# A residual block with attention and RWKV-7 time mixing: the recurrent part's two-operand multiplies move from GpSimd to VectorE, small copies to ScalarE, and the scheduler counts both

## The chip, the core and the metric

The kernel runs on one core of a Trainium2 chip. A core has five engines with queues of their own: TensorE (PE in the profile; PEld is its weight load), VectorE (DVE), ScalarE (ACT), GpSimd (POOL) and SyncE (SP), which here issues all DMA transfers. The metric is the device time of one execution in microseconds (us); smaller is better.

## The reference

One layer over 1024 tokens of 1024 channels, all in float32. The part that the change touches is the time mixing `rwkv7_time_mix`, 8 heads of 64 channels:

```python
def step(state, inp):                       # one token, one head
    r_t, w_t, k_t, v_t, kk_t, a_t = inp
    sa = einsum('bhvk,bhk->bhv', state, -kk_t)
    state = state * w_t + outer(sa, kk_t * a_t) + outer(v_t, k_t)
    return state, einsum('bhvk,bhk->bhv', state, r_t)

kk = k * k_k;  kk = kk / max(norm(kk), 1e-12)
k  = k * (1 + (a - 1) * k_a)
y  = (normalised scan output) * lnx_w + lnx_b
out = (y + bonus) * g
```

Around it stand a norm and an input projection, stick-breaking attention (8 heads; `q`, `k`, `v` from the same projection), sigmoid gates that merge the two branches, an output projection, and a SwiGLU FFN with 2816 hidden channels, each with a norm.

## The kernel before

Every matrix product is done as three products of float32r parts (high by high, high by low, low by high), so TensorE's work is large: most of it is a 128x128 weight block times 128x512 activations. Several products are done in Strassen's form, which adds sums of blocks on VectorE.

**The recurrence in chunks.** The 1024 tokens are cut into chunks of 64. Heads are handled in four pairs p (a pair fills 128 partitions) and the tokens in two halves hf of 8 chunks; one (p, hf) is called a unit here, and there are eight. For each unit `rw_elementwise` makes, on tiles of 128 partitions by 512 tokens, the running decay products `pp` and their inverses `pinv`, the normalised key `kk`, `ar` (kk and r times the decay) and `bk` (kk times a, and k', over the decay), and then the chunk matrices `nx` by small matmuls (64 rows by 128 columns; PE `e_e<-b_ar,b_bk`). Of each chunk a triangular 64x64 matrix has to be inverted, `rw_inverse`:

1. its 32x32 diagonal blocks go to DRAM (`nd`, 8 DMAs) and come back spread over partitions (`nl`);
2. VectorE inverts them in 16 pairs of a multiply and a reduce, the recursion (`b_tmp<-b_nl,q_q` and `q_q<-b_tmp`);
3. the result `ts` goes to DRAM in four DMAs (`td`) and comes back as `dn` (`q_q<-td`);
4. TensorE makes the off-diagonal block with two small products of 32x32 blocks, `ph` (`y_y<-q_q,b_nx`) and `pt` (`y_y<-q_q,q_q`); between them `ph` is copied from PSUM to `hb` (`COPY q_q<-y_y`).

I call these two the first and the second inverse product. `rw_chain` then carries the state from chunk to chunk: PE `c_c<-b_sv,b_nx`, ACT `b_xv<-c_c`, PE `c_c<-b_xv,b_bkt`, DVE `b_sv<-c_c,pl_pl,sp_sp`, where POOL makes `sp` (`sp_sp<-b_sv,pl_pl`, the decayed state) ahead of it. `rw_post` normalises a unit's output and multiplies it by the gate `g`. In attention, `values` makes differences `dv` of neighbouring values, and GpSimd masks each score block (`TENSOR_SCALAR_AFFINE_SELECT`) before VectorE's scan.

**Who sets the order.** Every operation is first recorded by `Block.record`, so the profile puts nearly all of them on one line, L610. Then `Block.schedule` simulates the five engines with a table of costs (`cost`), of latencies from engine to engine (`LATENCY`, and `MARGIN` for another engine), and of the times that transfers take beyond a fixed one (`LANDS`), and issues each engine's operations in the order that results. The chip keeps each engine's order and waits where the plan was wrong. Priorities are the order of recording with offsets: `CHAIN` for the state chain, `INV` for the inverse; projections of the next pair, attention and gates fill TensorE in between. `WB` and `PREFETCH` say how far ahead of its turn a tile may be granted. A two-input operation of VectorE or GpSimd on SBUF is made to end later when the other engine is in such an operation (`self.turn`); before, only `tensor_tensor` and `scalar_tensor_tensor` count.

Of the kernel before, what the change touches and what calls it, by code (L numbers as in the profile page):

```python
# [9 lines left out]
AF = mybir.ActivationFunctionType  # L10
ALU = mybir.AluOpType
# [4 lines left out]
P = 128  # L16
# [3 lines left out]
H = 512  # L20
# [12 lines left out]
WO_CLS = ("raw", "raw", "whi", "whi", "wlo", "wlo", "b", "b")  # L33
BY_OUT = (6, 5)
FIFTH = 0
INV = -100
AWAKE = (9, 8)
TQ = S // 4
POST = 0
# [2 lines left out]
SUMS_AT, OSPLIT = None, 1  # L42
MPS_A, MPS_S = "dydy", "ecec"
SBW = ("whi", "b", "wlo", "b")
WB, WP, WS, RB = 60, 8, 4, 2
PREFETCH = 14
CH = 64
RMS_EPS = 1e-6
GN_EPS = 64 * 1e-5
# [39 lines left out]
def is_ap(x):  # L89
    return hasattr(x, "tensor") and hasattr(x, "offset") and hasattr(x, "ap")  # L90
# [50 lines left out]
def cost(engine, method, kw, in_psum):  # L141

    out = kw.get("out", kw.get("ap"))
    if out is None:
        return 1283.0
    n = count(out.shape[1:])
    if engine == "tensor":
        if method == "transpose":
            return 2 + max(out.shape[0], n) / 1.2
        m, full = count(kw["lhsT"].shape[1:]), kw["lhsT"].dtype == F32  # L150
        if out.shape[0] <= CH and n <= CH:
            return 59.0 if out.shape[0] == CH else 27.0
        if full and kw["lhsT"].shape[0] == CH:
            return 122.0
        return 2 * (2 + max(m, n) / 1.2) if full else max(m / 2.4, 1.5 + 0.4435 * n)
    psum = any(is_ap(v) and k not in OUTS and in_psum(v) for k, v in kw.items())
    if engine == "vector":
        if method == "tensor_copy" and not psum:
            return 60 + 0.52 * n
        if method == "tensor_reduce":  # L160
            n = count(kw["in_"].shape[1:])
            return 64 + 1.042 * n
        if method == "scalar_tensor_tensor":
            return max(196, 68 + (1.16 if psum else 1.1) * n)
        if method == "tensor_tensor_scan":
            return 60 + 2.083 * n
        if method == "tensor_tensor" and abs(kw["in0"].ap[-1][0]) > 16:
            return 68 + 1.8 * n
        return 68 + 1.042 * n
    if engine == "scalar":  # L170
        extra = "accum_out" in kw or any(is_ap(kw.get(k)) for k in ("scale", "bias"))
        return 55 + 0.833 * n + (0 if psum else 40) + (90 if extra else 0)
    if engine == "gpsimd":
        if method == "memset":
            return 98 + 0.8 * n
        if method == "tensor_copy":
            return 180 + 3.4 * n
        if method == "tensor_scalar":
            return 320 + 2.4 * n
        return 150 + 2.1 * n  # L180
    size = 4 * count(out.shape)
    return max(450.0, size / 360.0)

LANDS = {"nd": -800.0, "nl": 1000.0, "td": -400.0, "tl": 800.0, "xv": 600.0, "spill": 1700.0, "gate": 2200.0, "act": 900.0, "x2": 1900.0, "orw": 1000.0, "w_rw": 1500.0, "w_sb": 1000.0, "w_fu": 1000.0, "w_fg": 500.0}


HELD, HEAD = 115.0, 140.0
POINTERS = ("scale", "bias", "scalar", "scalar1", "scalar2")  # L190
# [72 lines left out]
    "gpsimd": {"tensor": 155, "vector": 100, "scalar": 80, "gpsimd": 105, "sync": 60},  # L263
    "sync": {"tensor": 2030, "vector": 2030, "scalar": 2030, "gpsimd": 2060, "sync": 2030},
}
MARGIN = 80
CHAIN = -1000
SOON = -(10**7)

# [5 lines left out]
class Block:  # L275
# [150 lines left out]
    def schedule(self):  # L426

        import heapq

        for op in self.ops:  # L430
            op.ready = 0.0
            op.need = len(op.preds)
            op.left = op.need + len(op.tiles)
            for q in op.preds:
                q.succs.append(op)
        free = {e: 0.0 for e in ENGINES}
        self.begin, self.turn = {}, {}
        waiting = {e: [] for e in ENGINES}
        able = {e: [] for e in ENGINES}

        def release(op):
            ready = op.ready
            if op.bundle:
                op.bundle.left -= 1
                if op.bundle.left:
                    return
                ready = max(q.ready for q in op.bundle.ops)
                op = op.bundle.ops[0]
            heapq.heappush(waiting[op.engine], (ready, op.prio, op.seq, op))

        def advance(op):
            for q in self.want(op):
                release(q)

        for op in self.ops:
            if not op.left:
                release(op)
        for op in self.ops:
            if not op.need:
                advance(op)  # L460
        done = []
        last = None
        while len(done) < len(self.ops):
            best = None
            for e in ENGINES:
                if able[e]:
                    at = free[e]
                elif waiting[e]:
                    at = max(free[e], waiting[e][0][0])
                else:  # L470
                    continue
                if best is None or at < best[0]:
                    best = (at, e)
            if best is None:

                self.forced = False
                forced = [q for cls in self.places.values() for q in self.grant(cls, True)]
                assert self.forced, "the tiles do not fit"
                for q in forced:
                    release(q)  # L480
                continue
            at, e = best
            while waiting[e] and waiting[e][0][0] <= at:
                _, p, q, op = heapq.heappop(waiting[e])
                heapq.heappush(able[e], (p, q, op))
            op = self.choose(able[e], waiting[e], at, last)
            if op is None:
                free[e] = waiting[e][0][0]
                continue
            for op in op.bundle.ops if op.bundle else (op,):  # L490
                at, last = self.run(op, e, at, last, free, done, release, advance)
        return done
# [13 lines left out]
    def run(self, op, e, at, last, free, done, release, advance):  # L506
# [11 lines left out]
            last = op  # L518
        op.start = at
        op.end = at + op.cost  # L520
        if e in ("vector", "gpsimd") and op.method in ("tensor_tensor", "scalar_tensor_tensor") and not self.in_psum(op.kw["in0"]) and not self.in_psum(op.kw["in1"]):

            other = self.turn.get("gpsimd" if e == "vector" else "vector", 0.0)
            if other > at:
                op.end = max(op.end, other + op.cost - HEAD)
            self.turn[e] = op.end
        free[e] = op.end
        done.append(op)
        for q in op.succs:
            q.ready = max(q.ready, op.end + op.late + wait(e, q.engine))  # L530
# [6 lines left out]
        for tile in op.tiles:  # L537
            tile.left -= 1
            tile.ends[e] = max(tile.ends.get(e, 0.0), op.end)
            if not tile.left:  # L540
# [614 lines left out]
def rw_elementwise(b, u, p, hf, spill):  # L1155
    nc = b.nc
# [6 lines left out]
    def c8(t):  # L1163
        return t.rearrange("p (c t) -> p c t", c=8)
# [30 lines left out]
    ar = T("b", [P, 8, P], F32, "ar")  # L1195
    bk = T("b", [P, 8 * P], F32, "bk").rearrange("p (c a t) -> p c a t", c=8, a=2)
    nc.vector.scalar_tensor_tensor(out=ar[:, :, 0:CH], in0=c8(kk), scalar=-1.0, in1=pp[:, :, 0:CH], op0=ALU.mult, op1=ALU.mult)
    nc.gpsimd.tensor_tensor(out=ar[:, :, CH:P], in0=c8(r), in1=pp[:, :, 1 : CH + 1], op=ALU.mult)
    nc.gpsimd.tensor_tensor(out=kk[:], in0=kk[:], in1=a[:], op=ALU.mult)
    for h, rs in enumerate(halves):  # L1200
        nc.vector.tensor_tensor(out=bk[rs, :, h, :], in0=c8(kk)[rs], in1=c8(pinv)[rs], op=ALU.mult)

    nc.vector.tensor_scalar(out=a[:], in0=a[:], scalar1=pc(PC_KA + p), scalar2=oka[:, p : p + 1], op0=ALU.mult, op1=ALU.add)
    kp = a
    nc.gpsimd.tensor_tensor(out=kp[:], in0=k[:], in1=a[:], op=ALU.mult)
    for h, rs in enumerate(halves):
        nc.vector.tensor_tensor(out=bk[rs, :, 1 - h, :], in0=c8(kp)[rs], in1=c8(pinv)[rs], op=ALU.mult)

# [77 lines left out]
def rw_inverse(b, nd, nx, quads, tinit, p, hf):  # L1286

    nc = b.nc
# [42 lines left out]
        for c, h in ((c, h) for c in range(8) for h in range(2)):  # L1331
            nc.tensor.matmul(ph[bot[h], c, :], lhsT=nx[c // 4][top[h], c % 4, 0, h, 32:CH], rhs=dn[top[h], c, :], start=True, stop=True)
    for h in range(2):
        nc.vector.tensor_copy(hb[bot[h]], ph[bot[h]])
    pt = T("y", [P, 8, 32])
    with b.together():
        for c, h in ((c, h) for c in range(8) for h in range(2)):
# [47 lines left out]
def rw_post(b, y, u, p, hf, spill):  # L1385
    nc = b.nc
    T = b.t
    pc, ones = b.pc, b.ones
    t0 = T("b", [P, H], F32, "ptmp")
    nc.scalar.activation(t0[:], y[:], AF.Square)  # L1390
    pn = T("c", [P, H])
    nc.tensor.matmul(pn[:], lhsT=ones, rhs=t0[:], start=True, stop=True)
    rs = T("b", [P, H], F32, "ptmp")
    nc.scalar.activation(rs[:], pn[:], AF.Ln, scale=1.0 / CH, bias=b.eps[:, 1:2])
    nc.scalar.activation(rs[:], rs[:], AF.Exp, scale=-0.5)
    nc.vector.scalar_tensor_tensor(out=rs[:], in0=y[:], scalar=pc(PC_LW + p), in1=rs[:], op0=ALU.mult, op1=ALU.mult)
    nc.vector.scalar_tensor_tensor(out=rs[:], in0=rs[:], scalar=pc(PC_LB + p), in1=u["bv"][:], op0=ALU.add, op1=ALU.add)
    g = T("b", [P, H], F32, "ptmp")
    nc.sync.dma_start(g[:], spill["g"][:])
    b.ops[-1].late = LANDS["spill"]  # L1400
    nc.gpsimd.tensor_tensor(out=rs[:], in0=rs[:], in1=g[:], op=ALU.mult)
    nc.sync.dma_start(b.orw_d[p][:, hf * H : hf * H + H], rs[:])


# [19 lines left out]
def att_inputs(b, p):  # L1424
# [33 lines left out]
    def values():  # L1458
# [3 lines left out]
        for hf in range(2):  # L1462
# [6 lines left out]
            nc.scalar.copy(vt[:, 1 : H + 1], ps)  # L1469
            nc.gpsimd.tensor_copy(ends[0][:, 4 * hf : 4 * hf + 4], vt[:, P : H + 1 : P])  # L1470
            dv = T("b", [P, H], F32, "dv")
            nc.gpsimd.tensor_tensor(out=dv, in0=vt[:, 0:H], in1=vt[:, 1 : H + 1], op=ALU.subtract)
            pv = T("c", [P, 4, P])
            for i in range(4):
                nc.tensor.transpose(pv[:, i, :], dv[:, i * P : i * P + P], b.ident)
# [693 lines left out]
```

## Time and profile before

| | us |
|---|---|
| median of three runs (1549.14 to 1551.74) | 1549.5 |
| profiled execution, its own time | 1552.13 |
| its span, first to last instruction | 1550.3 |
| PE busy in the span | 1523.1 (98%) |
| DVE busy | 1290.0 (83%) |
| ACT busy | 795.1 (51%) |
| POOL busy | 218.2 (14%) |

The profiled execution lies 2.63 us above the median. A busy PE may still hold short waits between pipelined matmuls, so the rows on waits and the idle time ahead of single instructions say more than the 98%. By time: input norm to about 40 us, projections and the first units to 140, the recurrence with filler to about 440, attention to 640, then merge, output projection and FFN. Times in rows of the timeline are us from the span's start; what stands in brackets is the engine's idle time ahead of the row and what ended it.

### The profile page before, as it was taken

To read this page: it belongs to the slowest core of one execution; us is meant where nothing else is said; L and a number is where in the kernel's file an instruction comes from. 1 tells how busy PE (TensorE), PEld (TensorE's weight loads), DVE (VectorE), ACT (ScalarE), POOL (GpSimd) and SP (SyncE) were. 2 spreads that over 40 slices of the span, in tenths; PEclk is the share of its full clock that TensorE was granted. 3 is DMA by queue.
4 is the path that set the end of the run, shared out by engine and by line. 5 is a ranking of instruction groups with operands and counts; after the bars stand their busy time and mean duration, and the time that the engine had idled before them with its cause. 6 is when DMAs were issued, how large, how long until landed. Compare 5 with 4: busy or idle time off the path is not lost.

```text
span 1550.3 us, 24590 instructions
## 1 busy us (share of the span) xinstructions
PE 1523.1 (98%) x8957; PEld 1253.8 (81%) x8957; DVE 1290.0 (83%) x2218; ACT 795.1 (51%) x1623; POOL 218.2 (14%) x387
## 2 busy tenths in 40 slices
PE   8999999999999999999999999999999999999998
PEld 7877777778887888788888887888888888888886
DVE  7769898888686989985999789889889899976684
ACT  7634554555576677523656686233333334554351
POOL 1032355443523132000100000000000000000000
PEclk9999999999999999999999999999999999999999
DMA  9733332321010024543651532443232333964562
GB/s 363 265 92 83 90 101 75 100 83 49 28 42 27 28 68 144 189 142 125 211 170 58 194 135 71 148 166 119 76 129 83 110 115 118 351 217 130 166 214 109
DMA packets 116969, 200.88 MB, mean 130 GB/s; under 512 B 42992, under 2 KB 48368, under 8 KB 116848
## 3 DMA queue, kind: packets, MB, share of 16 engines
q1 hardware_dynamic: 116848, 199.30, 38.6%
q8 instruction: 71, 1.16, 0.3%
q14 instruction: 50, 0.41, 0.1%
HBM read 145.52 MB, written 51.64 MB: 127 GB/s over the span
## 4 chain that ended last, share of the span: by engine, by line
PE 84%; DVE 8%; DMA 3%; issue 2%; ACT 2%; POOL 1%; SPq 0%; DVEq 0%; POOLq 0%; ACTq 0%
PE d_d L610 27%; PE e_e L610 23%; PE c_c L610 18%; PE y_y L610 16%; DVE b_tmp L610 1%; DVE q_q L610 1%; DMA q_q<-td 1%; POOL sp_sp L610 1%; DVE big_h L610 1%; DVE b_xt L610 1%; DMA q_q<-consts 0%; DVE b_full L610 0%; SPq L610 0%; DMA b_nl<-nd 0%; DMA td<-q_q 0%
## 5 line engine op out<-in xcount | busy, mean ns | idle before, releaser
L610 PE MATMUL d_d<-big_h,whi_whi 128*128 128x512 f32 x832 | 286.1, 412 | 0.0
L610 PEld LDWEIGHTS d_d<-big_h,whi_whi 128*128 128x128 f32 x832 | 151.7, 189 | 30.1 <-issue 3.6
L610 PE MATMUL d_d<-big_h,wlo_wlo 128*128 128x512 f32 x416 | 170.1, 409 | 0.1
L610 DVE TENSOR_TENSOR_SCAN b_nb<-b_nb 128x128 f32<-128x128 f32 (+3 forms) x64 | 87.3, 1380 | 5.7 <-POOL b_nb L610 5.0
L610 PEld LDWEIGHTS d_d<-big_h,wlo_wlo 128*128 128x128 f32 x416 | 78.5, 189 | 16.1 <-issue 1.7
L610 POOL TENSOR_SCALAR sp_sp<-b_sv,pl_pl 64x64 f32<-64x64 f32 x120 | 71.7, 598 | 77.8 <-DVE b_sv L610 71.6
L610 PE MATMUL e_e<-big_h,b_a 128*128 128x512 f32 x264 | 67.6, 395 | 0.1
L610 PE MATMUL e_e<-big_h,whi_a 128*128 128x512 f32 x264 | 66.7, 395 | 0.8 <-ACT b_u L610 0.8
L610 PE MATMUL d_d<-b_wd,big_act 128*128 128x512 f32 x264 | 66.6, 394 | 0.0
L610 PE MATMUL e_e<-b_wd,big_act 128*128 128x512 f32 x264 | 66.3, 394 | 0.0
L610 PE MATMUL e_e<-big_h,wlo_a 128*128 128x512 f32 x264 | 66.1, 393 | 0.0
L610 ACT CAST b_wd<-b_wraw 128x512 fp32r<-128x512 f32 x65 | 38.1, 619 | 44.7 <-DVE b_wraw L610 22.9
L610 DVE TENSOR_TENSOR b_wt<-c_c,b_wt 128x512 fp32r<-128x512 f32 (+2 forms) x96 | 50.1, 546 | 10.5 <-ACT b_wt L610 8.9
L610 PEld LDWEIGHTS e_e<-b_wd,big_act 128*128 128x128 f32 x264 | 49.5, 188 | 11.5
L610 PEld LDWEIGHTS d_d<-b_wd,big_act 128*128 128x128 f32 x264 | 49.4, 188 | 11.5
L610 PEld LDWEIGHTS e_e<-big_h,whi_a 128*128 128x128 f32 x264 | 48.9, 188 | 12.0 <-ACT b_u L610 1.2
L610 PEld LDWEIGHTS e_e<-big_h,b_a 128*128 128x128 f32 x264 | 49.0, 188 | 11.6 <-ACT b_a L610 0.5
L610 PEld LDWEIGHTS e_e<-big_h,wlo_a 128*128 128x128 f32 x264 | 49.0, 188 | 10.5
L610 ACT COPY b_xv<-c_c 64x64 f32<-64x64 f32 x128 | 26.4, 206 | 57.5 <-PE c_c L610 56.2
L610 DVE TENSOR_TENSOR b_wd<-b_wraw,b_wd 128x512 fp32r<-128x512 f32 x65 | 42.3, 684 | 13.8 <-ACT b_wd L610 13.7
L610 PE MATMUL d_d<-big_h,whi_a 128*128 128x512 f32 x204 | 53.4, 398 | 0.0
L610 PE MATMUL d_d<-big_h,b_a 128*128 128x512 f32 x204 | 52.6, 397 | 0.4 <-ACT b_g L610 0.4
(898 smaller groups left out, 3982.4 us busy)
## 6 DMA issues: line engine op xcount, KB each, us to landing
raw_raw<-w_in SPq DMA_DIRECT2D x43, 512.0 KB, 3.8
raw_raw<-w_fg SPq DMA_DIRECT2D x26, 512.0 KB, 3.5
b_wraw<-w_fd SPq DMA_DIRECT2D x22, 512.0 KB, 4.8
act<-b_sa SPq DMA_DIRECT2D x32, 256.0 KB, 2.1
b_b<-w_fu SPq DMA_DIRECT2D x16, 512.0 KB, 4.3
b_x<-x SPq DMA_DIRECT2D x14, 512.0 KB, 6.3
act<-b_u SPq DMA_DIRECT2D x28, 256.0 KB, 2.3
raw_araw<-act SPq DMA_DIRECT2D x14, 512.0 KB, 4.0
```

Of the source, the lines that this page charges most:

```text
L610: getattr(getattr(self.real, op.engine), op.method)(**kw)
```

## The change

It does four things. The elementwise multiplies with two SBUF operands that GpSimd did in a unit (`ar`, `kk*a`, `k*a`), the last multiply of `rw_post` and the difference `dv` are issued on VectorE. A scaling of `a` by two per-partition numbers goes from VectorE to ScalarE, and so do the two `hb` copies of a unit. The planner's rule for GpSimd beside VectorE now also takes VectorE's scans as two-input operations and makes GpSimd's `tensor_scalar`, `tensor_copy` and `affine_select` end later beside one. SyncE's queue is modelled by an issue time (`ISSUE`) apart from the time in which transfers pass one after the other (`self.moved`). Some constants change with it.

```diff
-INV = -100
+INV = -300
-WB, WP, WS, RB = 60, 8, 4, 2
-PREFETCH = 14
+WB, WP, WS, RB = 50, 8, 4, 2
+PREFETCH = 13
...
         if method == "tensor_copy":
-            return 180 + 3.4 * n
+            return 180 + 0.84 * n
+        if method == "affine_select":
+            return 165 + n
...
-LANDS = {"nd": -800.0, "nl": 1000.0, "td": -400.0, "tl": 800.0, "xv": 600.0, ...
+LANDS = {"nd": -800.0, "nl": 1100.0, "td": -500.0, "tl": 800.0, "xv": 1050.0, ...
+ISSUE = {0.0: 500.0, LANDS["nd"]: 420.0, LANDS["td"]: 650.0, LANDS["xv"]: 750.0, LANDS["nl"]: 650.0}
...
-MARGIN = 80
+MARGIN = 100
...
-        if e in ("vector", "gpsimd") and op.method in ("tensor_tensor", "scalar_tensor_tensor") and not self.in_psum(op.kw["in0"]) and not self.in_psum(op.kw["in1"]):
-            other = self.turn.get("gpsimd" if e == "vector" else "vector", 0.0)
-            if other > at:
-                op.end = max(op.end, other + op.cost - HEAD)
-            self.turn[e] = op.end
+        if e in ("vector", "gpsimd"):
+            pair = self.paired(op)
+            if pair or e == "gpsimd" and op.method in ("tensor_scalar", "tensor_copy", "affine_select"):
+                other = self.turn.get("gpsimd" if e == "vector" else "vector", 0.0)
+                if other > at:
+                    op.end = max(op.end, other + op.cost - HEAD)
+                if pair:
+                    self.turn[e] = op.end
         free[e] = op.end
+        if e == "sync":
+            self.moved = max(self.moved, at) + op.cost
+            op.end = self.moved
+            free[e] = at + ISSUE.get(op.late, ISSUE[0.0])
...
+    def paired(self, op):
+        ins = [op.kw.get(k) for k in ("in0", "in1", "data0", "data1")]
+        return sum(is_ap(v) and not self.in_psum(v) for v in ins) == 2
...
-    nc.gpsimd.tensor_tensor(out=ar[:, :, CH:P], in0=c8(r), in1=pp[:, :, 1 : CH + 1], op=ALU.mult)
-    nc.gpsimd.tensor_tensor(out=kk[:], in0=kk[:], in1=a[:], op=ALU.mult)
+    nc.vector.tensor_tensor(out=ar[:, :, CH:P], in0=c8(r), in1=pp[:, :, 1 : CH + 1], op=ALU.mult)
+    nc.vector.tensor_tensor(out=kk[:], in0=kk[:], in1=a[:], op=ALU.mult)
...
-    nc.vector.tensor_scalar(out=a[:], in0=a[:], scalar1=pc(PC_KA + p), scalar2=oka[:, p : p + 1], op0=ALU.mult, op1=ALU.add)
+    nc.scalar.activation(a[:], a[:], AF.Identity, scale=pc(PC_KA + p), bias=oka[:, p : p + 1])
-    nc.gpsimd.tensor_tensor(out=kp[:], in0=k[:], in1=a[:], op=ALU.mult)
+    nc.vector.tensor_tensor(out=kp[:], in0=k[:], in1=a[:], op=ALU.mult)
...
-        nc.vector.tensor_copy(hb[bot[h]], ph[bot[h]])
+        nc.scalar.copy(hb[bot[h]], ph[bot[h]])
...
-    nc.gpsimd.tensor_tensor(out=rs[:], in0=rs[:], in1=g[:], op=ALU.mult)
+    nc.vector.tensor_tensor(out=rs[:], in0=rs[:], in1=g[:], op=ALU.mult)
...
-            nc.gpsimd.tensor_tensor(out=dv, in0=vt[:, 0:H], in1=vt[:, 1 : H + 1], op=ALU.subtract)
+            nc.vector.tensor_tensor(out=dv, in0=vt[:, 0:H], in1=vt[:, 1 : H + 1], op=ALU.subtract)
```

Since the order of every engine comes out of the plan, nearly all rows move. Three places are shown, all around the fifth unit (p = 2, hf = 0), which lies near 290 us in the profile before.

GpSimd there, before: `b_sh` is the tile of `tt`, `b_ptmp_3255` the output of `rw_post`, the other TENSOR_TENSOR rows are `ar`, `kk*a` and `k*a` of the last two units.

```order
L610 TENSOR_TENSOR b_ptmp_3255<-b_ptmp_3255,b_sh_1975 128x512
L610 COPY b_sh_2239<-q_q_3273 32x8x32 x3
L610 COPY pl_pl_3381<-b_pp_3253 128x8
L610 TENSOR_TENSOR b_ar_3444<-b_pp_2418,b_pp_3253 128x8x64
L610 TENSOR_TENSOR b_ar_3454<-b_tmp_1433,b_pp_3281 128x8x64
L610 TENSOR_TENSOR b_tmp_1433<-b_tmp_1433,b_pp_972 128x512
L610 TENSOR_SCALAR sp_sp_3495<-b_sv_2421,pl_pl_2459 64x64 x2
L610 TENSOR_TENSOR b_pp_972<-b_pp_972,b_tmp_3279 128x512
L610 TENSOR_SCALAR sp_sp_3517<-b_sv_2421,pl_pl_2459 64x64 x2
```

GpSimd at the same place, after:

```order
L624 COPY pl_pl_3199<-b_ptmp_976 128x8
L624 COPY carry_carry_3236<-b_ptmp_2312 128x1
L624 COPY b_a_662<-carry_carry_3236 128x1
L624 COPY b_ptmp_2304<-q_q_3266 32x8x32 x4
L624 MEMSET b_sv_3331 64x64 x2
L624 TENSOR_SCALAR sp_sp_3443<-b_sv_2607,pl_pl_2426 64x64 x2
```

The multiplies are gone from between the `sp` of the state chain: GpSimd's program goes from 44 TENSOR_TENSOR to 4.

VectorE there, before: the end of the next unit's recursion (`b_nl`), with the `hb` copies in it.

```order
L610 TENSOR_TENSOR b_tmp_2450<-b_nl_3073,q_q_2454 128x14x28
L610 COPY q_q_3384<-y_y_3311 32x256 x2
L610 TENSOR_REDUCE q_q_2454<-b_tmp_2450 128x7x2
L610 SCALAR_TENSOR_TENSOR b_pp_972<-b_pp_2418,par_par_158,b_pp_3253 128x512
L610 TENSOR_TENSOR b_tmp_2450<-b_nl_3073,q_q_2454 128x16x30
```

VectorE at the end of that recursion, after:

```order
L624 SCALAR_TENSOR_TENSOR b_ar_3245<-b_pp_2338,b_ptmp_976 128x8x64
L624 TENSOR_TENSOR b_sh_3028<-b_nl_3079,q_q_2364 128x14x28
L624 TENSOR_TENSOR b_pp_2338<-b_pp_2338,b_xl_600 128x512
L624 TENSOR_REDUCE q_q_2364<-b_sh_3028 128x7x2
L624 TENSOR_SCALAR b_sh_3028<-e_e_3408 128x512
L624 SCALAR_TENSOR_TENSOR b_sv_2607<-c_c_3420,pl_pl_2426,sp_sp_2863 64x64 x2
L624 TENSOR_TENSOR b_sh_3028<-b_nl_3079,q_q_2364 128x16x30
L624 TENSOR_TENSOR b_xl_600<-b_ptmp_2323,b_xl_600 128x512
```

The copies have left; the multiplies `kk*a` (`b_pp_2338`) and `k*a` (`b_xl_600`) stand between the steps of the recursion.

ScalarE and TensorE at the two inverse products, after; ScalarE first. `b_nx<-b_ar` are copies that may start only when the first inverse product has read `nx`.

```order
L624 COPY b_nx_2817<-b_ar_2441 64x4x64 x2
L624 COPY b_nx_2861<-b_ar_2441 64x4x64
L624 COPY q_q_3339<-y_y_3300 32x256 x2
L624 COPY b_xv_2686<-c_c_3337 64x64 x2
L624 COPY b_nx_2861<-b_ar_2441 64x4x64
```

```order
L624 MATMUL y_y_3300<-q_q_3266,b_nx_2861 32x32 x8
L624 MATMUL e_e_3293<-cst_cst_156,b_sh_2991 128x128
L624 MATMUL d_d_3286<-big_h_239,whi_whi_3178 128x512 x2
L624 MATMUL d_d_3286<-big_h_239,wlo_wlo_3225 128x512
L624 MATMUL c_c_3337<-b_sv_2607,b_nx_2817 128x128
L624 MATMUL d_d_3286<-big_h_239,whi_whi_3178 128x512 x2
L624 MATMUL d_d_3286<-big_h_239,wlo_wlo_3225 128x512
L624 MATMUL d_d_3286<-big_h_239,whi_whi_3178 128x512 x2
L624 MATMUL y_y_3353<-q_q_3339,q_q_3317 32x32 x16
```

The `hb` copies (`q_q_3339`) now stand in ScalarE's queue behind three of the `nx` copies, and eight products 512 wide lie between the two inverse products; before there are 23. Over the eight units these are 117 before and 54 after. Between a unit's last `nx` product and its first inverse product there are 1037 products 512 wide before, over the eight units, and 1021 after.

More of the change, by code (lines that the diff above doesn't have):

```diff
@@ L182, in cost @@
     return max(450.0, size / 360.0)
-LANDS = {"nd": -800.0, "nl": 1000.0, "td": -400.0, "tl": 800.0, "xv": 600.0, "spill": 1700.0, "gate": 2200.0, "act": 900.0, "x2": 1900.0, "orw": 1000.0, "w_rw": 1500.0, "w_sb": 1000.0, "w_fu": 1000.0, "w_fg": 500.0}
+LANDS = {"nd": -800.0, "nl": 1100.0, "td": -500.0, "tl": 800.0, "xv": 1050.0, "spill": 1700.0, "gate": 2200.0, "act": 900.0, "x2": 1900.0, "orw": 1000.0, "w_rw": 1500.0, "w_sb": 1000.0, "w_fu": 1000.0, "w_fg": 500.0}
+ISSUE = {0.0: 500.0, LANDS["nd"]: 420.0, LANDS["td"]: 650.0, LANDS["xv"]: 750.0, LANDS["nl"]: 650.0}
 HELD, HEAD = 115.0, 140.0
@@ L436, in schedule @@
         free = {e: 0.0 for e in ENGINES}
-        self.begin, self.turn = {}, {}
+        self.begin, self.turn, self.moved = {}, {}, 0.0
         waiting = {e: [] for e in ENGINES}
```

## The prediction

> **What bounds the kernel.** I read the page first: engines, then the chain that ended last, then the stretches of time, and there TensorE's waits.
>
> ```profile
> span 1550.3 us, 24590 instructions
> PE 1523.1 (98%) x8957; PEld 1253.8 (81%) x8957; DVE 1290.0 (83%) x2218; ACT 795.1 (51%) x1623; POOL 218.2 (14%) x387
> PE 84%; DVE 8%; DMA 3%; issue 2%; ACT 2%; POOL 1%; SPq 0%; DVEq 0%; POOLq 0%; ACTq 0%
> ```
> Stretch by stretch, the columns are the length and then the busy time of PE, PEld, DVE, ACT and POOL with their instructions, PE's granted clock, the share of the DMA engines and GB/s:
>
> ```profile
> 0.00:40.00 40.00, 34.58 (x236) 30.14 (x237) 31.97 (x65) 28.63 (x50) 7.08 (x20) 0.96 0.94 353
> 140.00:440.00 300.00, 290.15 (x2868) 233.61 (x2867) 250.46 (x532) 161.55 (x415) 140.31 (x251) 1.00 0.27 75
> 440.00:640.00 200.00, 195.58 (x1162) 167.09 (x1161) 174.32 (x230) 139.97 (x303) 45.06 (x67) 0.99 0.19 62
> 640.00:1325.00 685.00, 684.06 (x3252) 566.29 (x3251) 600.78 (x1037) 314.67 (x598) 6.45 (x4) 1.00 0.40 134
> 1325.00:1550.30 225.30, 218.80 (x964) 177.81 (x962) 158.69 (x237) 101.06 (x177) 0.00 (x0) 0.99 0.56 195
> ```
>
> TensorE bounds everything. The change leaves its instructions as they are, so only idle time can be won: 1550.3 - 1523.1 = 27.2 us. Of that 5.4 us lie in the first 40 us and 6.5 us after 1325 (the last results leaving), where the change moves nothing of weight. What is left is 9.9 us in the recurrence, 4.4 us in attention and 1.0 us elsewhere. VectorE is at 250 of 300 us in the recurrence, so it has room; GpSimd, idle by its total, is at 140 of 300 there.
>
> TensorE's waits by what ended them (total us, times, longest) say where the 15 us come from:
>
> ```profile
> PE c_c L610 <- DVE b_sv L610: 3.4, 4, 1.4
> PE y_y L610 <- DMA q_q<-td: 3.4, 3, 1.4
> PE y_y L610 <- DVE b_wt L610: 1.3, 2, 1.1
> PE y_y L610 <- DVE q_q L610: 1.3, 2, 1.1
> PE d_d L610 <- ACT b_g L610: 1.3, 2, 0.8
> PE e_e L610 <- ACT b_u L610: 0.8, 1, 0.8
> PE e_e L610 <- DVE q_q L610: 0.8, 1, 0.8
> PE e_e L610 <- DVE b_tmp L610: 0.7, 1, 0.7
> PE c_c L610 <- POOL b_nb L610: 0.6, 1, 0.6
> PE c_c L610 <- DVE b_nb L610: 0.5, 1, 0.5
> ```
>
> **Why GpSimd's multiplies are behind some of them.** Two places in the timeline, with TensorE's wait at the end of each:
>
> ```profile
> 288.75 1.58 DVE L610 TENSOR_TENSOR b_tmp<-b_nl,q_q 128x264 f32<-128x264 f32 x1
> 288.77 1.26 POOL L610 TENSOR_TENSOR b_ptmp<-b_ptmp,b_sh 128x512 f32<-128x512 f32 x1
> ...
> 295.62 0.86 DVE L610 COPY q_q<-y_y 32x256 f32<-32x256 f32 x2
> ...
> 296.63 0.69 PE L610 MATMUL y_y<-q_q,q_q 32*32 32x32 f32 x32 [1.09 <-DVE q_q L610]
> ```
> ```profile
> 334.22 1.65 DVE L610 TENSOR_TENSOR b_tmp<-b_nl,q_q 128x4 f32<-128x4 f32 x1
> 334.57 1.28 POOL L610 TENSOR_TENSOR b_sh<-b_sh,b_tmp 128x512 f32<-128x512 f32 x1
> ...
> 336.74 0.49 PE L610 MATMUL e_e<-b_ar,b_bk 64*128 64x128 f32 x4 [0.78 <-DVE q_q L610]
> ```
>
> A VectorE multiply of four elements a lane takes 1.65 us because a GpSimd multiply of 1.28 us runs beside it. Both engines lose, and all that stands behind in VectorE's queue is late: the `hb` copies at 295.62, for which TensorE waits 1.09 us. In the timeline I find 19 VectorE instructions longer than their kind beside such a GpSimd TENSOR_TENSOR; over the usual length they lose 14.8 us (the first and the last):
>
> ```profile
> 95.95 1.13 DVE L610 SCALAR_TENSOR_TENSOR b_ar<-b_r,b_sh 128x512 f32<-128x512 f32 x1
> ...
> 562.77 2.13 DVE L610 TENSOR_TENSOR b_a<-raw_raw,b_a 128x512 fp32r<-128x512 f32 x2
> ```
>
> **The change, part by part.** Durations for it, from the groups of instructions:
>
> ```profile
> L610 DVE TENSOR_TENSOR b_nl<-b_nl,b_tmp 128x512 f32<-128x512 f32 x4 | 2.7, 686 | 0.1
> L610 DVE TENSOR_SCALAR b_tmp<-b_tmp,par_par,small_small 128x512 f32<-128x512 f32 x2 | 1.1, 546 | 0.1
> L610 DVE COPY q_q<-y_y 32x256 f32<-32x256 f32 x16 | 6.8, 424 | 0.4
> ```
> ```profile
> L610 ACT COPY b_nx<-b_ar 64x256 f32<-64x256 f32 x32 | 12.9, 403 | 12.9 <-PE y_y L610 12.4
> L610 ACT COPY b_sh<-y_y 32x256 f32<-32x256 f32 x6 | 2.2, 364 | 2.4 <-PE y_y L610 2.3
> L610 ACT ACTIVATE b_sh<-c_c,small_small 128x512 f32<-128x512 f32 x2 | 1.4, 676 | 0.3 <-PE c_c L610 0.3
> ```
> ```profile
> L610 POOL TENSOR_SCALAR sp_sp<-b_sv,pl_pl 64x64 f32<-64x64 f32 x120 | 71.7, 598 | 77.8 <-DVE b_sv L610 71.6
> ```
>
> *VectorE's load.* It gains 40 operations (8 units with 3 multiplies, 8 last multiplies, 8 `dv`) of 0.686 us, 27.4 us. It loses 8 scalings of 0.546 (4.4 us) and the 16 `hb` copies (6.8 us). That is +16.2 us, against 14.8 us of stretching that ends: about even, +1.4 us. If a strided multiply ran like the stretched 1.13 us above, the 40 would cost 45 us; the unstretched 0.69 is nearer, as nothing on GpSimd with two operands is left beside it.
>
> *ScalarE's load.* 8 scalings at 0.676 (the nearest row with two pointer operands; it reads PSUM, and the 0.62 to 0.75 of its neighbours are the ends) and 16 copies at 0.364: 11.2 us, in a stage where ScalarE is busy 162 of 300 us.
>
> *Waits that go.* Those that I can follow back to a stretched instruction: the second inverse product (1.3), the small `nx` products at 336.74 (0.8), a norm product that waits for `b_tmp` (0.7), and a scan and a mask in attention, which I put down to `dv` beside them (0.6 and 0.5). Together -3.9 us. What is late next there is the filler itself, that is, nothing.
>
> *Waits for the inverse's transfers (3.4 us, three times).* From the first `td` store to the issue of `dn` takes 4.0 us where nothing else is queued (300.94 to 304.93):
>
> ```profile
> 300.94 2.52 SPq L610 DMA_DIRECT2D td<-q_q  x4
> 304.93 0.38 SPq L610 DMA_DIRECT2D q_q<-td  x1
> ```
> ```profile
> 288.49 0.69 PE L610 MATMUL y_y<-q_q,b_nx 32*32 32x32 f32 x32 [1.41 <-DMA q_q<-td]
> ```
>
> With the planner's 2.03 us for any transfer, the old constants allow 4 x 0.45 - 0.40 + 2.03 = 3.43 us for it, the new ones 3 x 0.65 + 0.45 - 0.50 + 2.03 = 3.93 us. So the plan puts the first inverse product 0.5 us later behind its stores, with other work ahead, and each of the three waits loses up to 0.5 us: -1.5 us. The ends are 0 (the waits come from other transfers in the queue) and -3.4 us.
>
> *Waits in the state chain (3.4 us, four times).* The plan now knows that `sp` on GpSimd waits for VectorE: its mean of 598 ns holds much of that. I take -1.0 us, between 0 (the order can't help) and -3.4 us.
>
> *New waits.* VectorE's queue holds 1.4 us more, and the `hb` copies stand behind up to four `nx` copies in ScalarE's queue. I take +1.5 us, between 0 and the price in the first rival. The remaining waits of 3.4 us (`b_wt`, `b_g`, `b_u`) I leave as they are; `PREFETCH`, `WB` and `MARGIN` alter the order in merge and FFN too, at 0 from a stage that loses 1.0 us in 685.
>
> Sum: -3.9 - 1.5 - 1.0 + 1.5 = -4.9 us. Against the profiled execution's 1552.13 us that is 1547.2 us; it lies 2.63 us above the median, so the forecast for the median is 1549.5 - 4.9 = 1544.6 us.
>
> **The rivals.** About 0.2% (3.1 us) is what a measurement of this kernel can tell from no change.
>
> *Slower: ScalarE comes too late for the second inverse product.* After the first product ScalarE has four `nx` copies (1.6 us), in two units an activation (0.68), and two `hb` copies (0.73) to do: 2.3 to 3.0 us. TensorE's filler there shrinks from 117 to 54 products 512 wide, six in most units. In the window 140 to 440 these stream at about 0.23 us each (four of them from 140.44 span under 1.1 us):
>
> ```profile
> 140.44 1.10 PE L610 MATMUL d_d<-big_h,whi_whi 128*128 128x512 f32 x4
> ```
>
> So six cover 1.4 us, and 1.6 us are uncovered at worst: 8 x 1.6 = 12.8 us, and 1549.5 - 4.9 + 12.8 = 1557.4 us. It decides from (4.9 + 3.1) / 8 = 1.0 us a unit on. Against it: in three of eight units only one or no `nx` copy stands ahead, and small products lie between too.
>
> *No change: VectorE's multiplies block GpSimd instead.* The row at 405.55 shows the other direction: two `sp` take 2.77 us beside a scan of 2.02 us.
>
> ```profile
> 405.55 2.77 POOL L610 TENSOR_SCALAR sp_sp<-b_sv,pl_pl 64x64 f32<-64x64 f32 x2
> 405.60 2.02 DVE L610 TENSOR_TENSOR_SCAN b_nb<-b_nb 128x896 f32<-128x896 f32 x1 [0.41 <-POOL b_nb L610]
> ```
>
> 32 multiplies of 0.686 us are 22 us, 7% of the recurrence. If 7% of the 120 `sp` meet one and lose half of it, that is 2.9 us on the state chain, at most all of it in TensorE's waits: 1549.5 - 4.9 + 2.9 = 1547.5 us, within 0.2%. Most steps of the chain have filler, which speaks against the full price. The Trainium skill, SBUF — State Buffer, "Who interferes with whom", has this rule: a VectorE instruction with two SBUF inputs contends with a GpSimd instruction that reads SBUF, and whichever starts first blocks the other fully. By that rule the move frees VectorE and leaves GpSimd's remaining reads with more instructions to wait for; the trace agrees in both directions (1.65 us for four elements, 2.77 us for two `sp`). By the rule taken alone the sum would be this rival's 1547.5 us, by the rows above 1544.6 us.
>
> *Much faster: nearly all waits between 40 and 1325 us go.* A plan that knows the contention and SyncE's queue could leave only a few: -12 us, 1537.5 us. Against it: the plan still mistakes single transfers by more than its margin of 0.1 us.
>
> That the change doesn't do what it says is excluded for the multiplies, since the order has 4 of 44 left on GpSimd.
>
> **How the numbers follow.** Forecast (gain of 3.1 to 9 us) 0.46, much faster 0.15, no change 0.22, slower 0.17. Faster by over 0.2% is 0.61, within it 0.22, slower 0.17. The likeliest case is 1544.6 us, by itself 1540.5 to 1546.4. The range goes from 1537.0, below the case of nearly all waits gone, to 1553.0, which leaves out the worse half of the slower case.
>
> **What would show it.** POOL busy near 160 us (218.2 less some 55), DVE within a few us of 1290, ACT near 806; no VectorE row of the recursion over 1.2 us; PE's waits on `DVE q_q` gone, on `q_q<-td` under 2 us in total. Wrong, if PE waits for `ACT q_q` ahead of the second inverse product by over 0.5 us in most units, if `c_c <- DVE b_sv` grows over 5 us, or if PE's idle time between 40 and 1325 us stays near 15 us.

## The result, and the profile after

The changed kernel takes 1541.7 us (median of 6 runs, 1540.74 to 1542.56) against 1550.41 us of the kernel before (6 runs, 1549.14 to 1551.74). The ratio is 0.9944, with a 95% interval of 0.9932 to 0.9957: 8.7 us faster. One of the eleven executions of run 1 below took 5310.61 us and is left out of that run's ratio and range. The forecast was 1544.6 us, in a range from 1537.0 to 1553.0.

The profiled execution took 1542.56 us (1552.13 before). Its page begins with the span and the engines; the third line is the chain that ended last:

```profile
span 1540.8 us, 24556 instructions
PE 1522.8 (99%) x8957; PEld 1254.1 (81%) x8957; DVE 1289.8 (84%) x2234; ACT 807.4 (52%) x1647; POOL 166.0 (11%) x347
PE 68%; DVE 10%; DMA 2%; issue 1%; ACT 1%; POOL 0%; SPq 0%; DVEq 0%; ACTq 0%
```

TensorE's work is the same (1522.8 us, 1523.1 before); its idle time fell from 27.2 to 18.0 us. The busy time by stage, with the columns that the prediction explained, tells where:

```profile
0.00:40.00 40.00, 34.80 (x218) 29.43 (x219) 31.81 (x63) 26.97 (x49) 5.65 (x17) 0.96 0.94 353
140.00:440.00 300.00, 298.45 (x2892) 241.71 (x2892) 252.46 (x532) 178.46 (x449) 108.76 (x225) 1.00 0.27 74
440.00:640.00 200.00, 198.28 (x1173) 169.82 (x1173) 178.05 (x243) 140.13 (x300) 35.74 (x58) 1.00 0.25 85
640.00:1315.50 675.50, 673.52 (x3207) 557.03 (x3206) 587.30 (x1018) 307.53 (x589) 6.48 (x4) 1.00 0.38 130
1315.50:1540.80 225.30, 217.81 (x954) 176.57 (x952) 158.59 (x238) 101.43 (x177) 0.00 (x0) 1.00 0.56 195
```

TensorE's idle time in the recurrence (140 to 440) went from 9.9 to 1.6 us, in attention from 4.4 to 1.7. After that it grew: from 1.0 to 2.0 us in merge and FFN, from 6.5 to 7.5 us in the last 225 us. TensorE's waits by what ended them, without those of the first 40 us, one of 1.1 us for the gates (`ACT b_g`, 1.3 before) and one of 0.4 us (`ACT b_u`):

```profile
PE d_d L624 <- ACT b_sa L624: 1.0, 2, 0.5
PE y_y L624 <- DVE b_u L624: 1.0, 1, 1.0
PE y_y L624 <- DMA q_q<-td: 0.7, 1, 0.7
PE y_y L624 <- DVE b_wt L624: 0.6, 2, 0.4
PE e_e L624 <- ACT b_a L624: 0.6, 1, 0.6
PE d_d L624 <- DVE b_r L624: 0.6, 1, 0.6
PE c_c L624 <- DVE b_sv L624: 0.3, 1, 0.3
```

The waits on `DVE q_q`, `b_tmp` and `b_nb` are gone, those on `q_q<-td` and `DVE b_sv` went from 3.4 us each to 0.7 and 0.3. The waits on `ACT b_sa`, `DVE b_u` and `ACT b_a`, all after 640 us, are new. What the moved work costs on ScalarE, and `sp` on GpSimd (598 ns before), by groups:

```profile
L624 ACT COPY q_q<-y_y 32x256 f32<-32x256 f32 x16 | 5.8, 364 | 0.6 <-POOL b_ptmp L624 0.4
L624 ACT ACTIVATE b_a<-b_a,small_small,par_par 128x512 f32<-128x512 f32 x4 | 3.3, 817 | 3.1 <-DVE b_sh L624 2.3 <-DVE b_sg L624 0.8
L624 POOL TENSOR_SCALAR sp_sp<-b_sv,pl_pl 64x64 f32<-64x64 f32 x120 | 67.6, 563 | 109.0 <-DVE b_sv L624 103.3
```

### The profile page after: what moved, and what is told of

The parts are those of the page before. It is cut to its first block, busy times and chain, and to the rows that moved or that the text cites. A ratio compares the mean times of both kernels' runs of the same rounds, so it can differ in the third digit from the quotient of the medians.

```text
span 1540.8 us, 24556 instructions
## 1 busy us (share of the span) xinstructions
PE 1522.8 (99%) x8957; PEld 1254.1 (81%) x8957; DVE 1289.8 (84%) x2234; ACT 807.4 (52%) x1647; POOL 166.0 (11%) x347
## 4 chain that ended last, share of the span: by engine, by line
PE 68%; DVE 10%; DMA 2%; issue 1%; ACT 1%; POOL 0%; SPq 0%; DVEq 0%; ACTq 0%
PE d_d L624 20%; PE e_e L624 19%; PE c_c L624 16%; PE y_y L624 13%; DVE b_u L624 2%; DVE b_sa L624 1%; DVE b_s L624 1%; DVE b_a L624 1%; DVE b_full L624 1%; DVE whi_a L624 1%; DVE wlo_a L624 1%; DMA act<-b_sa 1%; DVE b_tf L624 0%; DMA b_wraw<-w_fd 0%; DVE b_sh L624 0%
## 5 line engine op out<-in xcount | busy, mean ns | idle before, releaser
L624 POOL TENSOR_SCALAR sp_sp<-b_sv,pl_pl 64x64 f32<-64x64 f32 x120 | 67.6, 563 | 109.0 <-DVE b_sv L624 103.3
L624 DVE SCALAR_TENSOR_TENSOR b_sv<-c_c,pl_pl,sp_sp 64x64 f32<-64x64 f32 x120 | 33.8, 282 | 24.9 <-PE c_c L624 19.7
L624 ACT COPY b_xv<-c_c 64x64 f32<-64x64 f32 x128 | 26.4, 206 | 51.3 <-PE c_c L624 50.2
```

Of the source, the lines that this page charges most:

```text
L624: getattr(getattr(self.real, op.engine), op.method)(**kw)
```

## The experiments

Three theories were set against each other. A: the gain comes from ending the contention of GpSimd's multiplies with VectorE. B: it comes from a planner that counts what it left out. C: the order that any replanning makes is a new draw, and the one before was unlucky. (A fourth, D, arose on the way.)

All twelve in one table. "Stretch" is the time that VectorE's instructions take over the usual length (the 20th percentile) of their form (same operation, same shapes), summed over those that lose more than 0.15 us; idle times and busy time are TensorE's in the profiled execution.

| kernel | multiplies on | ratio to before (95%) | us | idle, recurrence | idle, all | PE busy | stretch |
|---|---|---|---|---|---|---|---|
| before | GpSimd | 1 | | 9.9 | 27.2 | 1523.1 | 16.8 |
| after | VectorE | 0.9944 (0.9932–0.9957) | -8.7 | 1.6 | 18.0 | 1522.8 | 3.5 |
| 1 order of before kept | VectorE | 0.9992 (0.9980–1.0005) | -1.2 | 5.5 | 22.2 | 1524.0 | 2.3 |
| 2 order of after kept | GpSimd | 0.9998 (0.9989–1.0007) | -0.3 | 5.3 | 23.6 | 1526.2 | 14.1 |
| 3 moves, old planner | VectorE | 0.9960 (0.9947–0.9973) | -6.2 | 4.9 | 19.3 | 1522.3 | 0.7 |
| 4 new planner, old engines | GpSimd | 0.9956 (0.9942–0.9969) | -6.8 | 1.6 | 19.4 | 1522.7 | 12.6 |
| 5 `MARGIN` 81 | GpSimd | 1.0005 (0.9996–1.0014) | +0.8 | 9.0 | 27.2 | 1522.4 | 17.7 |
| 6 GpSimd's rule alone | GpSimd | 1.0037 (1.0024–1.0051) | +5.7 | 9.6 | 28.0 | 1528.4 | 14.8 |
| 7 SyncE's model alone | GpSimd | 1.0020 (1.0011–1.0029) | +3.1 | 8.9 | 26.4 | 1524.4 | 15.0 |
| 8 multiplies alone, old planner | VectorE | 0.9956 (0.9942–0.9969) | -6.8 | 7.8 | 22.1 | 1522.3 | 2.3 |
| 9 after, old constants | VectorE | 0.9965 (0.9953–0.9978) | -5.4 | 0.7 | 20.9 | 1522.6 | 2.3 |
| 10 moves, old rules, new constants | VectorE | 0.9975 (0.9964–0.9986) | -3.9 | 5.0 | 22.3 | 1522.9 | 3.2 |
| 11 `INV`, `WB`, `PREFETCH` alone | GpSimd | 1.0014 (1.0001–1.0027) | +2.2 | 6.8 | 25.1 | 1528.9 | 17.9 |
| 12 as 4, `MARGIN` 101 | GpSimd | 1.0008 (0.9999–1.0018) | +1.2 | 7.3 | 24.1 | 1527.6 | 17.9 |

The us are (ratio - 1) x 1550, save for the kernel after, where the medians are compared.

### 1 and 2: the engine changed, the order kept

In the first the order of before is planned as before, and the five multiplies are issued on VectorE at their place; in the second that of after, with the multiplies issued on GpSimd.

```diff
     nc.gpsimd.tensor_tensor(out=kk[:], in0=kk[:], in1=a[:], op=ALU.mult)
+    b.ops[-1].to = "vector"        # in the second: planned on vector, to = "gpsimd"
...
-                getattr(getattr(self.real, op.engine), op.method)(**kw)
+                getattr(getattr(self.real, op.to), op.method)(**kw)
```

> The order of the kernel before is kept, instruction for instruction, and only the engine of the five multiplies changes when they are issued: GpSimd's TENSOR_TENSOR of a unit, the last multiply of the post step and `dv` go to VectorE at the same place of the order. The scaling and the `hb` copies stay on VectorE. Theory A (the gain comes from ending the multiplies' contention between GpSimd and VectorE, whatever the order): TensorE's waits on `DVE q_q` (2.1 us before), `DVE b_tmp` (0.7) and `b_nb` (1.1) go, those on `q_q<-td` and `DVE b_sv` (3.4 each) shrink a little: 3 to 6 us faster than before, about 1546 us. Theory B (the gain comes from the plan that counts what was left out): within 3 us of before (1550.4), since VectorE is handed 27 us of work that the order has no room for.

> The mirror image: the order of the changed kernel is kept, instruction for instruction, and only the five multiplies are issued on GpSimd again, at the same place of the order. Theory A: the stretching of VectorE returns (from 13.6 us to 25 us or more over the usual lengths) and with it 4 to 8 us of waits on VectorE's results: about 1547 us. Theory B: under 3 us slower than the changed kernel (1541.7), since the order and with it the td transfers stay where they are.

Measured: 1549.47 us against 1549.65 for the first (ratio 0.9992, no difference), 1550.07 us for the second (0.9998, the whole gain of after is lost). The second shows the contention at one place, with the same instructions in the same order. First after, then with the multiply back on GpSimd:

```profile
326.30 0.80 DVE L624 TENSOR_TENSOR b_xl<-b_xl,b_pp 128x512 f32<-128x512 f32 x1
327.02 0.15 DVE L624 TENSOR_TENSOR b_tmp<-b_nl,q_q 128x8 f32<-128x8 f32 x1
```
```profile
330.75 1.28 POOL L625 TENSOR_TENSOR b_xl<-b_xl,b_pp 128x512 f32<-128x512 f32 x1
330.81 1.25 DVE L625 TENSOR_TENSOR b_tmp<-b_nl,q_q 128x8 f32<-128x8 f32 x1
```

VectorE is through with both in 0.87 us (326.30 to 327.17); when GpSimd takes the multiply, VectorE is held for 1.25 us by eight elements a lane, and GpSimd's next `sp` comes after its own 1.28 us. The stretch rises from 3.5 to 14.1 us (the 13.6 us of the expectation are by another measure). TensorE's idle time rises from 18.0 to 23.6 us, in the recurrence from 1.6 to 5.3. Of the waits below, those on `b_sv` and `b_ptmp` lie in the recurrence, that on `b_nb` in attention, those on `b_a` near 946 and 1014 us:

```profile
PE c_c L625 <- DVE b_sv L625: 2.2, 3, 1.7
PE e_e L625 <- ACT b_a L625: 1.7, 2, 1.2
PE c_c L625 <- POOL b_ptmp L625: 0.8, 1, 0.8
PE c_c L625 <- DVE b_nb L625: 0.6, 1, 0.6
```

The second run thus lost the gain and got the stretch back, as A said, but contention isn't all that came back. The longest of these waits, 1.68 us, has another reason: VectorE sits idle for 2.87 us until GpSimd's multiply has ended, and `b_sv` stands behind the instruction that waits:

```profile
249.30 1.28 POOL L625 TENSOR_TENSOR b_xl<-b_r,b_xl 128x512 f32<-128x512 f32 x1
250.62 0.68 DVE L625 TENSOR_TENSOR b_bk<-b_xl,b_pp 64x512 f32<-64x512 f32 x1 [2.87 <-POOL b_xl L625]
251.97 0.46 PE L625 MATMUL c_c<-b_sv,b_nx 128*128 128x128 f32 x2 [1.68 <-DVE b_sv L625]
```

In the recurrence VectorE waits 9.7 us for results of GpSimd's TENSOR_TENSOR in run 2, none in the kernel after, 3.1 us before and 0 to 3.2 us in the kernels planned for GpSimd (4 to 7, 11 and 12). So run 2 shows what the multiplies on GpSimd cost in this order, through contention and late results together; it doesn't part the two. Of its 9.0 us longer span 3.4 us are busy time of TensorE (1526.2 against 1522.8), with a granted clock of 1.00 from 40 us to 1530 us in both; the reason for that part stays open.

For the first run, theory A was wrong: the stretch ends there too (2.3 us), the waits on `b_tmp` and `b_nb` go and those on `DVE q_q` and `q_q<-td` fall to 0.6 and 1.0, but the median doesn't move. VectorE has 260 of 300 us in the recurrence instead of 250, in an order that was not made for it, and the waits of the state chain stay at 3.6 us, now seven; in six of them `b_sv` starts within 0.03 us of the end of the VectorE instruction ahead of it, that is, VectorE was busy until then:

```profile
140.00:440.00 300.00, 294.48 (x2890) 236.07 (x2889) 259.74 (x560) 165.25 (x423) 110.55 (x227) 1.00 0.27 75
```
```profile
PE c_c L611 <- DVE b_sv L611: 3.6, 7, 1.1
```

The profiled execution (1547.99 us) has 5.0 us less idle time than before, and one run took 1544.67; others took up to 1553.91. Why this kernel scatters over 9 us, where after scatters over 2, isn't seen in one profile and stays open.

### 3 and 4: the moves without the planner, the planner without the moves

The third is the kernel before with the moves of the change (all lines with `nc.vector` and `nc.scalar` in its diff), the fourth the changed kernel with those lines undone.

> The kernel before with all of the moves (five multiplies to VectorE, the scaling and the `hb` copies to ScalarE), planned anew by the old planner with its old costs and constants. Theory A: most of the gain is there, 1543 to 1546 us, with td waits as before (2 to 4 us). Theory B: 1548 to 1551 us, PE idle in the recurrence 7 us or more (9.9 before, 1.6 after), td and `b_sv` waits together over 4 us.

> The changed kernel's planner, costs and constants, with every operation on the engine that it had before. Theory A: 1547 to 1551 us: the plan now knows when a multiply on GpSimd is blocked, but the time is lost all the same. Theory B: 1541 to 1545 us, with td waits under 1.5 us and `b_sv` under 1.5 us as in the changed kernel. If A and B add (each half), this and the run of the moves alone each lie near 1546 us.

Measured: 1544.13 us (ratio 0.9960) and 1543.73 us (0.9956). Each alone has about three quarters of the gain, so neither A nor B is right by itself, and they don't add: -6.2 and -6.8 against -8.7 us together. The recurrence, third kernel first:

```profile
140.00:440.00 300.00, 295.15 (x2905) 238.81 (x2904) 251.49 (x538) 180.06 (x455) 108.06 (x227) 0.99 0.27 75
```
```profile
140.00:440.00 300.00, 298.44 (x2904) 242.60 (x2903) 255.64 (x530) 171.18 (x433) 136.13 (x251) 1.00 0.27 76
```

In the fourth GpSimd still works 136 us there and VectorE is still stretched by 12.6 us, but TensorE waits only 1.6 us. Was that the plan's knowledge, or a lucky order? The next runs take the plan apart.

### 5 to 8: a control, the planner's two rules, the multiplies alone

```diff
5: -MARGIN = 80
   +MARGIN = 81
6: +            pair = self.paired(op)     # with the costs of tensor_copy and affine_select
7: +            self.moved = max(self.moved, at) + op.cost     # with ISSUE and LANDS
8: -    nc.gpsimd.tensor_tensor(...)       # five lines
   +    nc.vector.tensor_tensor(...)
```

> A control: the kernel before with `MARGIN = 81` instead of 80, 1 ns in the planner's latencies and nothing else. The order of the operations changes all the same. Theory B (the plan knows something that is true of the chip): no change, 1548 to 1552 us, PE idle in the recurrence 7 to 12 us. Rival C (any new order is a new draw, and the kernel before was an unlucky one, so that every replanned kernel lies lower): 1542 to 1547 us here too, as the runs of the moves alone (1544.1) and of the planner alone (1543.7).

> The kernel before with one part of the planner's change: the rule for GpSimd beside VectorE (scans count as two-input operations, GpSimd's tensor_scalar, tensor_copy and affine_select end later beside one) with the costs of GpSimd's copies and masks. Engines, SyncE's model and constants as before. Theory B: this is the part that matters for `DVE b_sv`, `DVE q_q` and attention: 1544 to 1546 us, PE idle in the recurrence under 5 us (9.9 before), `b_sv` under 1.5, attention's idle under 3 us (4.4 before), td waits still 2 us or more. Rival (SyncE's model carries the gain): 1548 us or more. Rival C: 1542 to 1547 with no pattern in what goes.

> The kernel before with the other part of the planner's change: SyncE's queue by issue time and moving time (`ISSUE`, `moved`) and the new `LANDS`. Engines, GpSimd's rule and constants as before. Theory B: td waits fall from 3.4 us to under 1.2 us and nothing else in particular: 1546.5 to 1548.5 us, `b_sv` still 2 us or more. Rival (SyncE's model carries the gain): 1544 us or less. Rival C: 1542 to 1547 with no pattern in what goes.

> The kernel before with the five multiplies on VectorE, planned anew by the old planner; the scaling and the `hb` copies stay on VectorE, whose queue in the recurrence holds 11 us more than in the run of all the moves (1544.1 us). Theory A: the multiplies carry the gain of the moves: 1543 to 1546 us, `DVE q_q`, `b_tmp` and `b_nb` waits gone. Rival (the small copies carry it, by making room on VectorE): 1548 us or more, with PE waiting for `DVE q_q` ahead of the inverse products.

Measured: 1551.43 us (no difference), 1557.06 (slower), 1553.41 (slower) and 1543.66 (ratio 0.9956, as fast as all moves). The control speaks against C in its simple form. Both rules alone cost time, which no theory had. SyncE's model does what it says at its place, and the time is given back elsewhere:

```profile
PE c_c L616 <- DVE b_sv L616: 3.6, 5, 1.1
PE c_c L616 <- ACT whi_a L616: 3.1, 1, 3.1
PE c_c L616 <- ACT b_xv L616: 2.4, 3, 0.9
PE y_y L616 <- DMA q_q<-td: 0.5, 1, 0.5
```

The waits for `td` fell from 3.4 to 0.5 us; 3.1 us for `whi_a` and 2.4 for `b_xv` came. GpSimd's rule alone left `b_sv` at 3.4 us. Its loss isn't idle time (28.0 us against 27.2) but busy time, 1528.4 us against 1523.1; the last section shows from what.

The multiplies alone carry the gain of the moves, as theory A has it, with td (3.1 us) and `b_sv` (3.2 us) as they were. Of the idle time that goes, 3.3 us lie in attention (4.4 to 1.1) and only 2.0 in the recurrence:

```profile
440.00:640.00 200.00, 198.86 (x1186) 170.57 (x1185) 178.16 (x244) 142.15 (x306) 38.84 (x61) 1.00 0.22 73
```
```profile
PE c_c L610 <- DVE b_sv L610: 3.2, 4, 1.1
PE y_y L610 <- DMA q_q<-td: 3.1, 3, 1.8
```

### 9 to 11: the constants

Theory D: the constants carry the planner's share.

```diff
9:  -INV = -300; WB = 50; PREFETCH = 13; MARGIN = 100     # in the changed kernel
    +INV = -100; WB = 60; PREFETCH = 14; MARGIN = 80
10: +INV = -300; WB = 50; PREFETCH = 13; MARGIN = 100     # in the kernel before, with the moves
11: +INV = -300; WB = 50; PREFETCH = 13                   # in the kernel before
```

> The changed kernel with the old constants (`INV` -100, `WB` 60, `PREFETCH` 14, `MARGIN` 80); its engines, its rule for GpSimd beside VectorE and its model of SyncE's queue stay. Theory D (the constants carry the planner's share, the new rules by themselves cost, as the runs of either rule alone did with +5.8 and +3.1 us): 1545 us or more, with PE idle in the recurrence over 4 us. Rival (rules carry it on the new engines): within 2 us of the changed kernel, 1540 to 1543.5 us.

> The kernel before with all of the moves and the new constants, but the old rules: GpSimd's sp, copies and masks are not counted beside VectorE, and SyncE's queue is modelled as before. Theory D: 1540 to 1543 us, as fast as the changed kernel, and under the moves alone (1544.1). Rival (the rules carry it): 1544 us or more.

> The kernel before with `INV` -300, `WB` 50 and `PREFETCH` 13 alone; engines, rules and `MARGIN` as before (with `MARGIN` 100 the old engines and rules give no plan whose tiles fit). Theory D: 1543 to 1546.5 us, most of what the whole new plan gives on the old engines (1543.7). Rival (rules and constants only work together): 1548 us or more.

Measured: 1545.16, 1546.14 and 1552.56 us. D falls: the constants alone gain nothing on either set of engines (2.2 us slower on the old, and on the new 0.9975 against 0.9960 without them). In the ninth the time matches D but not its reason: the recurrence is nearly without idle time (0.65 us), and the loss lies in attention, idle 4.45 us, with one wait of 3.3 us:

```profile
140.00:440.00 300.00, 299.35 (x2945) 243.95 (x2944) 258.30 (x549) 183.95 (x460) 111.28 (x229) 1.00 0.27 76
440.00:640.00 200.00, 195.55 (x1143) 166.37 (x1142) 177.98 (x242) 137.49 (x293) 32.40 (x58) 1.00 0.24 84
```
```profile
PE e_e L624 <- DVE b_g L624: 3.3, 1, 3.3
```

### 12: was the fourth a good draw?

```diff
-MARGIN = 100
+MARGIN = 101
```

> A control on the one kernel that was faster with GpSimd's multiplies left where they were: the whole new planner and its constants with the old engines (1543.7 us), with `MARGIN` 101 instead of 100. Nothing that the plan knows differs, but the order of the operations changes. If the new plan as a whole is worth some 6 us on the old engines: 1542 to 1546 us again, PE idle in the recurrence under 3 us (1.6 there). If that run was one good order among many: 1547 us or more, PE idle in the recurrence over 5 us, as in the four other plans with the old engines.

Measured: 1552.23 us, ratio 1.0008, no difference from before. One nanosecond in the planner's latencies takes the whole 6.8 us of the fourth run away, and waits are back. Between the two profiled executions lie 4.7 us of idle time and 4.9 us of busy time; in run 12 the granted clock is at half for 6.8 us from 352.7 us on:

```profile
140.00:440.00 300.00, 292.74 (x2868) 235.66 (x2867) 256.50 (x539) 163.32 (x418) 136.57 (x251) 0.99 0.27 73
```
```profile
PE c_c L624 <- DVE b_sv L624: 3.7, 3, 1.3
```

So the new plan doesn't bring the gain by its knowledge alone: one order that it makes has it, the neighbouring one hasn't. Two orders can't say which is the usual one, but with the runs before them the fast one is the exception. **What the twelve say together:** of the kernels with the multiplies on GpSimd that were planned for it, five of six lie between +0.8 and +5.7 us and one at -6.8. All five with the multiplies on VectorE and a plan made for it (3, 8, 9, 10 and after) are faster, by 3.9 to 8.7 us, whatever rules and constants the planner had. The multiplies are the cause, on condition that the order is made for them (run 1). How much of it is the end of the contention, and how much that VectorE no longer waits for results from GpSimd, isn't parted (run 2 has both). The planner's part isn't shown: with the moves on board, the old planner gained 6.2 us and the new one or parts of it 3.9 to 8.7, which is the scatter of the orders. The changed kernel itself was not run with a nudged `MARGIN`, so whether its 8.7 us are usual for its plan is open.

## Why the prediction was right

*The bound.* Right: TensorE's busy time stayed, and 9.2 us of idle time went. Of it 8.3 us came from the recurrence and 2.7 from attention, the two stages named.

*The load of the engines.* VectorE ended at 1289.8 us (1290.0 before; forecast +1.4), so the 16.2 us of new work did go into room that was there: the stretch fell by 13.3 us by the measure of the table, and the other 3 us are not followed. ScalarE gained 12.3 us instead of 11.2: the scaling takes 0.82 us, not the 0.68 of the row that I chose as nearest, which has one per-partition operand (the bias) and not two, as I wrote. GpSimd is at 166 us (about 160 forecast).

*Waits that go, -3.9 us.* As forecast: `DVE q_q`, `b_tmp` and `b_nb` fell to nothing, and no VectorE row of the recursion between 140 and 440 us is longer than 0.69 us. Run 8 shows that the multiplies alone do this.

*The td transfers, -1.5 us.* Mis-sized: -2.7 us. The model of SyncE does work there by itself (3.4 to 0.5 us in run 7), but the multiplies moved in the kept order of before already brought 3.4 to 1.0 us (run 1), without the constants that my reason needed. And by itself it wasn't worth its size: run 7 ended 3.1 us slower all the same.

*The state chain, -1.0 us.* Mis-sized, at -3.1 us, and the reason isn't borne out: with GpSimd's rule alone `b_sv` stayed at 3.4 us, and in run 12 it was 3.7 us with the whole new plan. What took these waits away in the changed kernel stays open; with the moves and the old planner (run 3) they were 1.6 us.

*New waits, +1.5 us.* None on `ACT q_q`, and 0.6 us (`b_r`) in the recurrence. The step that put merge and FFN at 0 was wrong: about 2 us came there and in the last stage (`b_sa`, `b_a`, `b_u`). With the true sizes the sum is -3.9 - 2.7 - 3.1 + 0.6 + 2.0 = -7.1 us; `b_wt` (1.3 to 0.6) is part of the rest to -9.2, the remainder lies in waits too short to follow singly.

*The rivals.* The slower one (ScalarE late for the second inverse product) didn't come: no such wait. "No change" named something that the trace shows, VectorE's instructions holding GpSimd's, but the moved multiplies didn't add to it: `sp` took 563 ns in the mean instead of 598, and GpSimd's rows together lost 45 us over their usual lengths (51 before, by the measure of the table). TensorE's waits for `b_sv` were 0.3 us, not the 2.9 us of this rival on top. The rule named from the Trainium skill, SBUF — State Buffer, "Who interferes with whom", agrees with the pair of rows of run 2. The result lies at the upper end of the forecast's case (gain of 3.1 to 9 us), towards "nearly all waits go". That it lies in the case of the forecast is more than luck, since all five kernels with the multiplies on VectorE and a plan made for it do (3.9 to 8.7 us); its place among them is not, as two terms were too small by 3.3 us together and the sum still misses 2.1 of 9.2 us.

*What I had not asked* is how much a plan of this kind scatters. Orders that differ by one nanosecond in a latency lie 8 us apart (runs 4 and 12), as much as the whole gain, about half of it through idle time and half through a lowered clock; that belonged in the range as a term of its own.

## What to carry to other kernels

A two-operand multiply on GpSimd can hold a two-operand instruction of VectorE for its own length, even one of eight elements a lane (1.25 us beside 1.28 us). VectorE does the multiply in 0.7 us instead of 1.3, and 40 of them, 27.4 us, raised its busy time by only 6.2 us (run 8) to 9.4 us (run 1). TensorE gained from that only where the order was planned again. Where a planner sets the order, a change to it should be tried with a neutral nudge beside it before a cause is named: here a single good run had looked like proof of a better model. And a wait that is taken away is worth its size only if the new order brings no others, as run 7 showed.

## What the runs showed of the hardware

Idle time can cost TensorE twice. In run 6 TensorE is busy for 1.42 us of the 4 us after 340, and its granted clock then falls to half for some 7 us (the columns are the length, PE busy, the granted clock, the DMA share and GB/s):

```profile
338.00:340.00 2.00, 2.00 (x13) 1.00 0.14 49
340.00:342.00 2.00, 0.96 (x5) 1.00 1.03 303
342.00:344.00 2.00, 0.46 (x2) 1.00 0.70 173
344.00:346.00 2.00, 1.70 (x6) 0.79 0.22 84
346.00:348.00 2.00, 1.23 (x4) 0.50 0.14 51
348.00:350.00 2.00, 1.56 (x5) 0.50 0.22 49
350.00:352.00 2.00, 2.00 (x7) 0.50 0.58 217
```
```profile
343.17 0.46 PE L619 MATMUL c_c<-b_sv,b_nx 128*128 128x128 f32 x2 [1.89 <-DVE b_sv L619]
344.29 0.47 PE L619 MATMUL d_d<-big_h,whi_whi 128*128 128x512 f32 x1 [0.66 <-DVE b_kst L619]
```

The longest gap there is 1.89 us. The Trainium skill, TensorE: Matmul & The Clock Gate, "HAM oscillation — how this bites in real kernels", sets the limit at idle gaps of more than about 3.4 us; here a shorter gap with smaller ones around it was enough. A single gap of 1.79 us was followed by half the clock in run 8 (first two rows below), while in run 7 a gap of 3.08 us, with 0.91 us of work in four, was not (last two rows; the clock stayed at 1.00 after them). So what decides isn't settled by these runs.

```profile
144.00:146.00 2.00, 0.33 (x20) 1.00 0.80 213
146.00:148.00 2.00, 2.00 (x28) 0.53 0.00 0
```
```profile
648.00:650.00 2.00, 0.60 (x3) 1.00 0.80 310
650.00:652.00 2.00, 0.31 (x1) 1.00 0.03 11
```

The lost clock counts as busy time: runs 6, 11 and 12 have 1527.6 to 1528.9 us of it against 1523.1. In run 6 the clock is at half for 17.1 us in all up to 1530 us, before for 6.8 us; at half speed the 10.3 us more are up to 5.1 us of lost work (an estimate), nearly all of the 5.3 us by which its busy time is longer. In the changed kernel no stretch of 10 us between 20 and 1530 us had a granted clock under 0.99; before, one had 0.83, at 470 us.
